# Weighted values of an attention kernel in 24 closed runs, and its output projection in three groups of rows

## The chip, the cores and the metric

The kernel runs on one core of a Trainium2 chip. Its engines are TensorE (PE for matrix products, PEld for the loads of their stationary operand), VectorE (DVE), ScalarE (ACT), GpSimd (POOL) and SyncE (SP, which issues most DMAs). Each executes its own queue in the order in which it was written, and engines wait for each other by semaphores. The metric is the device time of one execution in microseconds; smaller is better.

## The reference

Two layers of a decoder trunk over 512 tokens and 1024 features in float32. A layer is a gated feed-forward block, a mixer, and a second feed-forward block. The mixer's input projection feeds three groups of heads, whose outputs are concatenated and projected:

```python
x = x + 0.5 * swiglu(rmsnorm(x, ffn1_norm[l]), ...)
z = rmsnorm(x, mix_norm[l]) @ w_in[l]
y_s5, y_hg = s5_mixer(...), hgrn2_mixer(...)        # 256 + 256 columns
y_nsa = nsa_mixer(q_nsa, kv_nsa, gate_nsa, ...)     # 512 columns, 8 heads of 64 in 2 groups
y = jnp.concatenate([y_s5, y_hg, y_nsa], axis=-1)
x = x + y @ w_out[l]
x = x + 0.5 * swiglu(rmsnorm(x, ffn2_norm[l]), ...)
```

In `nsa_mixer` each block of 128 queries has three attentions (compressed keys, selected keys, a window), each softmax(q k + bias) times v, added with gates. With 512 tokens selection and window cover every earlier token, so both are causal attentions over blocks of 128 keys.

## The kernel before

Dense products keep precision by splitting: `mm3` (L222 to L226) makes a product of 128 by 512 from three matmuls, high weights times high input (L224), high weights times low input (L225), low weights times high input (L226). `wload` fetches a weight piece by an SP DMA into one of four `wraw` buffers; `wsplit` casts its high part on ACT (L218) and subtracts for the low part on DVE (L219), three buffers each. Products collect in PSUM tiles with the tag `pd`, of which there are two.

The program is written by Python generators which a small `Weave` interleaves; the framework's scheduler then orders the instructions of each engine. In `mixer`, `dense()` makes the input projection and starts the three head groups as their inputs come up; `outs()` works as filler beside them.

The attention is `nsa`. It has 16 units: group g (2), head pair hp (2) and query block i (4, of i+1 key blocks). I call the four units of one (g, hp) a half of a group. Each unit has three steps, and step `turn` comes two units behind `scores`, step `mix` three units behind (`LAG`):

- `scores`: four pairs of score matmuls into PSUM tiles with the tag `pS`, two buffers (L1154, L1155); on DVE bias plus minimum, L1158; on ACT exp, L1162; on DVE four small operations and the scaling by gate over sum, L1169.
- `turn`: i+1 transposes `ppt` for each of four probability tiles (L1178), and an ACT copy of each tile to `PT` (L1180).
- `mix`: 4(i+1) matmuls `pno` of values by transposed probabilities (L1194). Each uses 128 by 64 of the array and gives 64 rows; head e = 0 and e = 1 go to the two halves of the columns. After i = 3 one full matmul adds the compressed attention (L1197, called `pno.c` below), and `split` casts the half's output to its high part on ACT (L969) and takes the low part on DVE (L970). They are entries 4 to 7 of `self.y`; 0 and 1 come from the S5 heads, 2 and 3 from HGRN2.

The output projection `wout` goes over groups of entries of `self.y`, `WP = ((0, 1, 2, 3), (4, 5, 6, 7))`. For each of eight output tiles m it loads the piece of W for the group, makes three matmuls for each entry and adds PSUM to `x` on DVE (L1359). `outs` runs all groups but the last beside the head groups, each once its entries exist. The last runs when all generators are done, and also makes the next norm's sums and inputs (`norm_x`).

Of the kernel before, what the change touches and what calls it, by code (L numbers as in the profile page):

```python
# [19 lines left out]
L, DM, FF, DEPTH = 512, 1024, 2816, 2  # L20
# [37 lines left out]


GAP = 99.0  # L60


class Trunk:
# [13 lines left out]
    SB = (1.0, 1.5)  # L77
    S0 = 1
    ORD = ('h0', 'i', 's', 'h1', 'k0', 'v', 'c', 'k1')
    WP = ((0, 1, 2, 3), (4, 5, 6, 7))  # L80
    WW = 0.333
    CMPU = 2
    NW, HW, SW = 1.176, 0.84, 1.2
# [1038 lines left out]
    def nsa(self, st):  # L1122

        nc = self.nc
        v = nc.vector
        V, gates = st["v"], st["g"]
        T, pcT, po = {}, {}, {}
        units = [(g, hp, i) for g in range(2) for hp in range(2) for i in range(4)]

        def start(g):  # L1130
            while "k%d" % g not in st:
                yield 1.0
            T[g] = [self.bias_tile(4 * g + r) for r in range(4)]

        def cmp(g):
            while "vc" not in st:
                yield 1.0
            pcT[g] = yield from self.nsa_cmp(g, T[g], st["k%d" % g][1], st["kc"], gates)

        def scores(g, hp, i):  # L1140

            h = 4 * g + 2 * hp
            KS, Q = st["k%d" % g]
            n = 128 * (i + 1)
            nm = max(n, 256)
            qs = slice(i * 128, (i + 1) * 128)
            mx, sm_ = self.s([128, 4], "mx"), self.s([128, 4], "smx")
            P = [None] * 4
            for b in range(2):
                kh, kl = KS[b]  # L1150
                ps = [self.pmt(name="psS", tag="pS") for _ in range(2)]
                for e in range(2):

                    nc.tensor.matmul(ps[e][:, :nm], Q[2 * hp + e][:, qs], kh[:, :nm], start=True, stop=False)  # L1154
                    nc.tensor.matmul(ps[e][:, :nm], Q[2 * hp + e][:, qs], kl[:, :nm], start=False, stop=True)  # L1155
                for e in range(2):
                    p = P[2 * e + b] = self.t2(name="P")
                    v.tensor_tensor_reduce(p[:, :n], T[g][2 * hp + e][:, L - n:], ps[e][:, :n], 1.0, 1e29, OP.add,  # L1158
                                           OP.min, mx[:, 2 * e + b:2 * e + b + 1])
                yield 0.25 + 0.15 * i  # L1160
            for j in range(4):
                nc.scalar.activation(P[j][:, :n], P[j][:, :n], AF.Exp, bias=mx[:, j:j + 1], scale=-1.0,  # L1162
                                     accum_out=sm_[:, j:j + 1])
            v.tensor_scalar(sm_[:], sm_[:], TINY, None, op0=OP.max)
            v.reciprocal(sm_[:], sm_[:])
            v.tensor_tensor(sm_[:].rearrange("p (e b) -> p e b", e=2), sm_[:].rearrange("p (e b) -> p e b", e=2),
                            gates[:, i, 3 * h:3 * h + 6].rearrange("p (e k) -> p e k", e=2)[:, :, 1:3], op=OP.mult)
            for j in range(4):
                v.tensor_scalar(P[j][:, :n], P[j][:, :n], sm_[:, j:j + 1], None, op0=OP.mult)  # L1169
            return P  # L1170

        def turn(i, P):
            R = []
            n = 128 * (i + 1)
            for k in range(4):
                pt = self.pmt(name="ppt", tag=("pS", "pv")[k % 2])
                for j in range(i + 1):
                    nc.tensor.transpose(pt[:, j * 128:(j + 1) * 128], P[k][:, j * 128:(j + 1) * 128], self.idn[:])  # L1178
                PT = self.t2(name="PT")
                nc.scalar.copy(PT[:, :n], pt[:, :n])  # L1180
                R.append(PT)
                if k % 2:
                    yield 0.2 * (i + 1)
            return R

        def mix(g, hp, i, R):
            if i == 0:
                po[0] = self.pmt(name="pno", tag="po")
            qs = slice(i * 128, (i + 1) * 128)
            for b in range(2):  # L1190
                for j in range(i + 1):
                    c = slice(g * 128 + 64 * b, g * 128 + 64 * b + 64)
                    for e in range(2):
                        nc.tensor.matmul(po[0][64 * e:64 * e + 64, qs], V[:, j, c], R[2 * e + b][:, j * 128:(j + 1) * 128],  # L1194
                                         start=i == 0 and b == 0, stop=False, skip_group_check=True)
            if i == 3:
                nc.tensor.matmul(po[0][:], st["vc"][g][:, hp], pcT[g][:], start=False, stop=True, skip_group_check=True)  # L1197
                self.y[4 + 2 * g + hp] = self.split(po[0][:])
        P, R = {}, {}
        n = len(units)  # L1200
        lt, lm = self.LAG
        yield from start(0)
        nxt = {}
        for g in range(2):
            nxt[8 * g + self.CMPU] = cmp(g)
        nxt[self.K1] = start(1)
        run = []
        for k in range(n + lm):
            if k in nxt:
                run.append((k, nxt[k]))  # L1210
            for j, q in list(run):
                for _ in range(1 if k < j + 2 else 10 ** 6):
                    try:
                        yield next(q)
                    except StopIteration:
                        run.remove((j, q))
                        break
            if k < n:
                P[k] = yield from scores(*units[k])
            if 0 <= k - lt < n:  # L1220
                R[k - lt] = yield from turn(units[k - lt][2], P.pop(k - lt))
            if 0 <= k - lm < n:
                mix(*units[k - lm], R.pop(k - lm))
                yield 0.44 * (units[k - lm][2] + 1)


    def dense_tok(self, W, n, name, gates=None):
# [43 lines left out]
    def mixer(self, l, gi_next):  # L1271
        nc, A = self.nc, self.A
        with self.tc.tile_pool(name="mp%d" % l, bufs=self.NB) as mp:
# [29 lines left out]
                yield from self.s5_glu(l, y2)  # L1303

            def outs(n):
                for cs in self.WP[:n]:
                    while any(self.y[c] is None for c in cs):
                        yield 1.0
                    yield from self.wout(l, cs)

            def dense():
                for it in self.ORD:
# [30 lines left out]
            W.add(outs(len(self.WP) - 1), self.WW)  # L1343
            W.run()
            self.norm_start()
            drain(self.wout(l, self.WP[-1], True, gi_next))
        self.norm_end()

    def wout(self, l, cs, last=False, gi_next=None):
        nc = self.nc  # L1350
        n = len(cs)
        assert cs == tuple(range(cs[0], cs[0] + n))
        for m in range(KT):
            h, lo = self.wload(self.A["wo"][l, m][:, cs[0] * 128:(cs[0] + n) * 128], n * 128)
            ps = self.pmt(name="pd", tag="pd")
            for j, c in enumerate(cs):
                sl = slice(j * 128, (j + 1) * 128)
# [32 lines left out]
def _layout(inp):  # L1390
    a = {k: np.asarray(v) for k, v in inp.items()}
    r = {}
# [36 lines left out]
        return c(w.reshape(DEPTH, 128, KT * len(cols_)))  # L1429
    r["wvi"] = tok(HI + ar(256))  # L1430
    r["wvn"] = tok(np.concatenate([kvc(j, g) for g in range(2) for j in (3, 5)] + [GT + ar(24)]))
    r["wo"] = c(np.stack([tiles(a["w_out"][l], 128) for l in range(DEPTH)]).reshape(DEPTH, KT, 128, 1024))

    def cat(u, w):
        return np.concatenate([u, w], 0)
# [58 lines left out]
```

## Time and profile before

| | |
|---|---|
| median of 3 runs (range) | 2086.31 us (2082.22 to 2089.9) |
| profiled execution, its own time | 2082.53 us |
| its span | 2080.8 us |
| PE busy | 2051.0 us, 99% of the span |
| DVE, ACT busy | 57%, 38% |
| granted TensorE clock | 0.996 of full speed |

The span is the time from the first to the last instruction of the profiled execution; 1.7 us of its own time lie outside. Busy time is the union of an engine's instructions. PE matmuls are pipelined and their ends are modelled, so starts are more reliable than durations: what a matmul costs is read from its start to the start of the next one. A matmul of float32 operands with a 64-column array tile shows as two records; an average line can hide a stretch with other limits, so the stretches are read one by one.

### The profile page before, as it was taken

The page shows a single profiled execution, that of the slowest core. Times are in us where ns is not written, and L with a number is a line of the kernel's source. Part 1 is how long each engine was busy: PE and PEld are TensorE (multiplying, and loading weights), DVE is VectorE, ACT ScalarE, POOL GpSimd, SP SyncE. Part 2 cuts the span into 40 slices and gives each one's busy share as a digit, 9 for nine tenths or more (in the row PEclk, how much of TensorE's full clock was granted, in tenths as well). Part 3 has the DMA queues.
Part 4 walks back from the last instruction along what each step waited for, and adds up shares of the span by engine and source line. Part 5 has one row for each costly group of instructions (what it writes and reads, how often), then busy time and mean ns, then how long its engine had stood idle before and what let it go on. Part 6 is the DMA issues. An engine that isn't in the chain of part 4 may idle for free.

```text
span 2080.8 us, 28931 instructions
## 1 busy us (share of the span) xinstructions
PE 2051.0 (99%) x11192; PEld 1686.2 (81%) x11192; DVE 1188.5 (57%) x2653; ACT 782.2 (38%) x1455; POOL 83.4 (4%) x153
## 2 busy tenths in 40 slices
PE   8999999999999999999999999999999999999997
PEld 6888888877877888888888888888787778888886
DVE  7865545677776864543544344356777764344445
ACT  5322323445666332222332223234456663222221
POOL 1000000111000100000000000001110000000000
PEclk9999999999999999999999999999999999999999
DMA  5334433432102433432333233234221023233322
GB/s 194 110 103 138 133 130 94 151 126 97 52 26 63 142 114 94 151 95 80 110 101 89 84 114 99 80 105 151 99 97 52 32 87 91 86 97 112 97 78 69
DMA packets 69753, 209.11 MB, mean 100 GB/s; under 512 B 9272, under 2 KB 11912, under 8 KB 69616
## 3 DMA queue, kind: packets, MB, share of 16 engines
q1 hardware_dynamic: 58192, 172.19, 26.9%
q0 software_dynamic: 11280, 35.05, 4.9%
q8 instruction: 88, 1.44, 0.3%
q14 instruction: 49, 0.40, 0.1%
q10 hardware_dynamic: 144, 0.03, 0.0%
HBM read 194.63 MB, written 15.22 MB: 101 GB/s over the span
## 4 chain that ended last, share of the span: by engine, by line
PE 96%; DVE 2%; issue 0%; DMA 0%; ACT 0%; POOL 0%; SPq 0%; DVEq 0%; ACTq 0%
PE pd L224 27%; PE pd L226 27%; PE pd L225 27%; PE pno L1194 2%; PE ppt L1178 2%; PE psS L1154 1%; PE psS L1155 1%; PE pd L1246 1%; PE pd L1247 1%; PE pd L1248 1%; PE psc L1092 1%; PE plv L876 1%; PE pno L1197 0%; PE pho L942 0%; PE pY L784 0%
## 5 line engine op out<-in xcount | busy, mean ns | idle before, releaser
L218 ACT CAST whi<-wraw 128x1024 fp32r<-128x1024 f32 (+5 forms) x377 | 345.3, 918 | 1020.5 <-PE pd L225 713.8
L224 PE MATMUL pd<-xs,whi 128*128 128x512 f32 x1664 | 655.9, 394 | 9.6 <-ACT whi L218 6.1
L226 PE MATMUL pd<-xs,wlo 128*128 128x512 f32 x1664 | 652.0, 392 | 0.0
L225 PE MATMUL pd<-xs,whi 128*128 128x512 f32 x1664 | 650.4, 391 | 0.0
L219 DVE TENSOR_TENSOR wlo<-wraw,whi 128x1024 fp32r<-128x1024 f32 (+5 forms) x377 | 396.8, 1054 | 144.2 <-ACT whi L218 135.3
L224 PEld LDWEIGHTS pd<-xs,whi 128*128 128x128 f32 x1664 | 313.6, 188 | 77.2 <-ACT whi L218 6.1
L226 PEld LDWEIGHTS pd<-xs,wlo 128*128 128x128 f32 x1664 | 313.4, 188 | 65.4
L225 PEld LDWEIGHTS pd<-xs,whi 128*128 128x128 f32 x1664 | 313.5, 188 | 63.8 <-DVE xs L164 0.7
L224 PE MATMUL pd<-hb,whi 128*128 128x512 f32 x682 | 265.8, 390 | 0.0
L226 PE MATMUL pd<-hb,wlo 128*128 128x512 f32 x682 | 265.4, 389 | 0.0
L225 PE MATMUL pd<-hb,whi 128*128 128x512 f32 x682 | 265.4, 389 | 0.0
L293 DVE TENSOR_TENSOR ft<-ft,pd 128x512 f32<-128x512 f32 x88 | 60.5, 687 | 247.3 <-PE pd L226 247.0
L287 DVE TENSOR_TENSOR ft<-pd,rbc 128x512 f32<-128x512 f32 x88 | 60.7, 690 | 188.8 <-PE pd L226 188.8
L226 PEld LDWEIGHTS pd<-hb,wlo 128*128 128x128 f32 x682 | 128.0, 188 | 26.6
L225 PEld LDWEIGHTS pd<-hb,whi 128*128 128x128 f32 x682 | 128.1, 188 | 26.4
L224 PEld LDWEIGHTS pd<-hb,whi 128*128 128x128 f32 x682 | 128.1, 188 | 26.3
L312 DVE TENSOR_TENSOR ft<-pd,r 128x512 f32<-128x512 f32 x62 | 42.9, 692 | 109.7 <-PE pd L226 109.4
L1162 ACT ACTIVATE P<-P,mx 128x128 f32<-128x128 f32 (+3 forms) x128 | 71.4, 559 | 36.2 <-DVE mx L1158 35.0
L1158 DVE CUSTOM_DVE_ANT_0 P<-Tb,psS 128x128 f32<-128x128 f32 (+3 forms) x128 | 60.3, 483 | 21.0 <-PE psS L1155 20.1
L295 DVE TENSOR_TENSOR hb<-ft,hb 128x512 fp32r<-128x512 f32 x88 | 60.3, 685 | 0.0
L288 ACT ACTIVATE ft<-ft 128x512 f32<-128x512 f32 x88 | 55.1, 628 | 12.8 <-DVE ft L287 12.5
L294 ACT CAST hb<-ft 128x512 fp32r<-128x512 f32 x88 | 54.7, 622 | 13.0 <-DVE ft L293 11.1
(388 smaller groups left out, 2138.6 us busy)
## 6 DMA issues: line engine op xcount, KB each, us to landing
wraw<-in_gu SPq DMA_DIRECT2D x175, 512.0 KB, 3.5
wraw<-in_dn SPq DMA_DIRECT2D x64, 384.0 KB, 3.0
wraw<-in_dn SPq DMA_DIRECT2D x64, 320.0 KB, 2.8
wraw<-in_win SPq DMA_DIRECT2D x32, 512.0 KB, 3.6
w<-sp POOLq DMA_DIRECT2D x32, 256.0 KB, 5.7
wraw<-in_wo SPq DMA_DIRECT2D x32, 256.0 KB, 2.6
Tb<-tbl POOLq DMA_DIRECT2D x16, 256.0 KB, 4.2
tbl<-ext POOLq DMA_DIRECT2D x1, 2560.0 KB, 20.5
```

Of the source, the lines that this page charges most:

```text
L218: nc.scalar.copy(h[:, sl], w[:, sl])
L219: self.mark = nc.vector.tensor_tensor(lo[:, sl], w[:, sl], h[:, sl].bitcast(F32), op=OP.subtract)
L224: nc.tensor.matmul(ps, wh, xh, start=first, stop=False)
L225: nc.tensor.matmul(ps, wh, xl, start=False, stop=False)
L226: nc.tensor.matmul(ps, wl, xh, start=False, stop=last)
L287: nc.vector.tensor_tensor(t[:], pg[:], rbc[:], op=OP.mult)
L288: nc.scalar.activation(t[:], t[:], AF.Silu)
L293: nc.vector.tensor_tensor(t2[:], t[:], pu[:], op=OP.mult)
L294: nc.scalar.copy(hb[:, 0, f], t2[:])
L295: nc.vector.tensor_tensor(hb[:, 1, f], t2[:], hb[:, 0, f].bitcast(F32), op=OP.subtract)
L1158: v.tensor_tensor_reduce(p[:, :n], T[g][2 * hp + e][:, L - n:], ps[e][:, :n], 1.0, 1e29, OP.add, OP.min, mx[:, 2 * e + b:2 * e + b + 1])
L1162: nc.scalar.activation(P[j][:, :n], P[j][:, :n], AF.Exp, bias=mx[:, j:j + 1], scale=-1.0, accum_out=sm_[:, j:j + 1])
```

## The change

It has two parts.

1. `mix` now takes its `pno` matmuls in one closed run. Blocks i = 0 and 1 of a half go together (12 matmuls), i = 2 (12) and i = 3 (16) alone, so there are three runs in each of four halves of two layers. The matmuls have high priority in the scheduler, and a dependency without a semaphore orders the first behind all ACT copies of the run. Blocks 0 and 1 share their four `PT` tiles.
2. The output projection has three groups, `((0, 1), (4, 5), (2, 3, 6, 7))`, and the rows of its weights are stored in that order. The first needs the S5 heads alone, the second the attention's group 0; the last group keeps four entries.

```diff
-    WP = ((0, 1, 2, 3), (4, 5, 6, 7))
+    WP = ((0, 1), (4, 5), (2, 3, 6, 7))
...
         def turn(i, P):
...
+            o = 128 if i == 1 else 0
+            if i != 1:
+                PT[:] = [self.t2(name="PT") for _ in range(4)]
...
-                PT = self.t2(name="PT")
-                nc.scalar.copy(PT[:, :n], pt[:, :n])
-                R.append(PT)
+                c = nc.scalar.copy(PT[k][:, o:o + n], pt[:, :n])
+                R.append((PT[k], o, c.ins.name))
...
-        def mix(g, hp, i, R):
+        def mix(g, hp, blocks):
...
+            with self.tc.high_priority():
+                for i, R in blocks.items():
...
+                                mm.append(nc.tensor.matmul(po[0][64 * e:64 * e + 64, qs], V[:, j, c],
...
+                for R in blocks.values():
+                    for _, _, c in R:
+                        self.tc.add_manual_dep(mm[0].ins, c, NOSYNC, reason="one run")
...
-            if 0 <= k - lm < n:
-                mix(*units[k - lm], R.pop(k - lm))
-                yield 0.44 * (units[k - lm][2] + 1)
+            if 0 <= k - lm < n and units[k - lm][2]:
+                g, hp, i = units[k - lm]
+                bl = (0, 1) if i == 1 else (i,)
+                mix(g, hp, {j: R.pop(k - lm + j - i) for j in bl})
+                yield 0.44 * sum(j + 1 for j in bl)
...
-    def wout(self, l, cs, last=False, gi_next=None):
+    def wout(self, l, q, last=False, gi_next=None):
...
+        cs = self.WP[q]
+        n, o = len(cs), sum(len(g) for g in self.WP[:q])
         for m in range(KT):
-            h, lo = self.wload(self.A["wo"][l, m][:, cs[0] * 128:(cs[0] + n) * 128], n * 128)
+            h, lo = self.wload(self.A["wo"][l, m][:, o * 128:(o + n) * 128], n * 128)
```

The diff does not show where the scheduler puts the instructions. In the rows below `psS` are score matmuls (`kh` the first of a pair, `kl` the second), `ppt` transposes, `pno` matmuls of values, `pd<-y` the output projection, `psc` scores of the compressed attention; `x4` is the number of equal instructions in a row. The changed kernel's lines are some 1 to 20 further down: L1154 and L1155 become L1155 and L1156, L1178 becomes L1183, L1194 becomes L1203, L1197 becomes L1211.

The first place is PE in the second half of group 0, layer 0. Before:

```order
L1194 MATMUL pno<-PT,vn 64x128
L1178 MATMUL ppt<-idn,P 128x128 x8
L1194 MATMUL pno<-PT,vn 64x128 x11
L1092 MATMUL psc<-kc,q 128x7 x4
L1178 MATMUL ppt<-idn,P 128x128
L1194 MATMUL pno<-PT,vn 64x128
L226 MATMUL pd<-y,wlo 128x512
L1154 MATMUL psS<-kh,q 128x384
L1155 MATMUL psS<-kl,q 128x384
L1178 MATMUL ppt<-idn,P 128x128
L1194 MATMUL pno<-PT,vn 64x128 x2
```

The same half now, at its first run (the fourth of the layer's twelve):

```order
L1156 MATMUL psS<-kl,q 128x512
L1183 MATMUL ppt<-idn,P 128x128 x4
L225 MATMUL pd<-y,whi 128x512
L226 MATMUL pd<-y,whi 128x512
L227 MATMUL pd<-y,wlo 128x512
L1203 MATMUL pno<-PT,vn 64x128 x12
L1155 MATMUL psS<-kh,q 128x256
L1156 MATMUL psS<-kl,q 128x256
```

Pieces of one to eleven `pno` between other matmuls became one run of twelve, five rows behind the last score matmul of block 3.

The second place is ACT in the same half, whose copies the run needs. Before:

```order
L1162 ACTIVATE P,smx<-P,mx 128x512 x4
L1180 COPY PT<-ppt 128x256 x4
L218 CAST whi<-wraw 128x512
L1162 ACTIVATE P,smx<-P,mx 128x128 x4
L1180 COPY PT<-ppt 128x384 x4
```

Now:

```order
L219 CAST whi<-wraw 128x256
L1163 ACTIVATE P,smx<-P,mx 128x512 x4
L1184 COPY PT<-ppt 128x256 x2
L1163 ACTIVATE P,smx<-P,mx 128x128 x4
L1184 COPY PT<-ppt 128x384 x4
L1163 ACTIVATE P,smx<-P,mx 128x256 x4
L1184 COPY PT<-ppt 128x512 x4
```

The order of exps and copies on ACT hardly moved: two of the four copies of 256 columns, all four of 384 and all four of 512 still stand behind four exps of a later block.

The third place is PE at the end of the attention, layer 0. Before:

```order
L224 MATMUL pd<-y,whi 128x512
L225 MATMUL pd<-y,whi 128x512
L1178 MATMUL ppt<-idn,P 128x128 x12
L1194 MATMUL pno<-PT,vn 64x128 x8
L1178 MATMUL ppt<-idn,P 128x128 x16
L1194 MATMUL pno<-PT,vn 64x128 x28
L1197 MATMUL pno<-pcT,vc 128x512
L226 MATMUL pd<-y,wlo 128x512
```

Now:

```order
L1155 MATMUL psS<-kh,q 128x512
L1156 MATMUL psS<-kl,q 128x512
L1183 MATMUL ppt<-idn,P 128x128 x4
L1203 MATMUL pno<-PT,vn 64x128 x12
L1183 MATMUL ppt<-idn,P 128x128 x12
L1203 MATMUL pno<-PT,vn 64x128 x12
L1183 MATMUL ppt<-idn,P 128x128 x10
L1203 MATMUL pno<-PT,vn 64x128 x16
L1211 MATMUL pno<-pcT,vc 128x512
L225 MATMUL pd<-y,whi 128x512 x2
```

The 28 `pno` behind 16 transposes became runs of 12 and 16, each right behind transposes, and the first run stands four transposes behind the last score matmul.

## Rows read from the trace of the kernel before

**Rows 1.** The page's head and part 1: busy time, share of span, instructions.

```profile
span 2080.8 us, 28931 instructions
...
PE 2051.0 (99%) x11192; PEld 1686.2 (81%) x11192; DVE 1188.5 (57%) x2653; ACT 782.2 (38%) x1455; POOL 83.4 (4%) x153
```

**Rows 2.** Windows: stretch, length, busy us of PE, PEld, DVE, ACT, POOL, clock, DMA.

```profile
540.00:660.00 120.00, 120.00 (x852) 93.44 (x850) 82.79 (x355) 77.53 (x258) 2.14 (x4) 1.00 0.11 35
...
584.05:606.24 22.19, 22.19 (x175) 17.18 (x174) 16.65 (x69) 14.98 (x50) 0.00 (x0) 1.00 0.06 22
```

**Rows 3.** Waits of PE, longest in total first: us, times, longest.

```profile
PE pd L224 <- ACT whi L218: 6.1, 1, 6.1
```

**Rows 4.** Timeline of PE around two runs of values: start us, us, instruction.

```profile
561.91 0.28 PE L1154 MATMUL psS<-kh,q 128*128 128x256 f32 x1
562.03 0.28 PE L1155 MATMUL psS<-kl,q 128*128 128x256 f32 x1
562.24 1.09 PE L1194 MATMUL pno<-PT,vn 128*64 128x128 f32 x14
563.26 0.50 PE L224 MATMUL pd<-y,whi 128*128 128x512 f32 x1
563.60 0.40 PE L225 MATMUL pd<-y,whi 128*128 128x512 f32 x1
563.84 0.40 PE L226 MATMUL pd<-y,wlo 128*128 128x512 f32 x1
...
566.69 0.43 PE L1194 MATMUL pno<-PT,vn 128*64 128x128 f32 x2
567.05 0.50 PE L224 MATMUL pd<-y,whi 128*128 128x512 f32 x1
```

**Rows 5.** Timeline, the last block of the attention: last score, fourth exp, first copy.

```profile
646.45 0.39 PE L1155 MATMUL psS<-kl,q 128*128 128x512 f32 x1
...
647.64 0.71 ACT L1162 ACTIVATE P<-P,mx 128x512 f32<-128x512 f32 x1
...
648.35 0.35 ACT L1180 COPY PT<-ppt 128x256 f32<-128x256 f32 x1
```

**Rows 6.** Groups by line and shape: count | busy us, mean ns | idle before.

```profile
L1180 ACT COPY PT<-ppt 128x512 f32<-128x512 f32 x32 | 16.4, 597 | 1.8 <-PE ppt L1178 1.8
...
L1180 ACT COPY PT<-ppt 128x384 f32<-128x384 f32 x32 | 13.0, 493 | 0.1
...
L1180 ACT COPY PT<-ppt 128x256 f32<-128x256 f32 x32 | 10.0, 371 | 3.8 <-PE ppt L1178 3.8
```

**Rows 7.** Timeline, a block of 256 keys: last score, fourth exp, copies behind it.

```profile
575.22 0.28 PE L1155 MATMUL psS<-kl,q 128*128 128x256 f32 x1
...
576.05 0.49 ACT L1162 ACTIVATE P<-P,mx 128x256 f32<-128x256 f32 x1
...
576.54 2.03 ACT L1180 COPY PT<-ppt 128x512 f32<-128x512 f32 x4
```

**Rows 8.** Timeline, a block of 128 keys: last score and fourth exp.

```profile
571.07 0.28 PE L1155 MATMUL psS<-kl,q 128*128 128x256 f32 x1
...
571.94 0.39 ACT L1162 ACTIVATE P<-P,mx 128x128 f32<-128x128 f32 x1
```

**Rows 9.** Timeline of PE, the last 16 transposes and the 28 `pno` behind.

```profile
651.26 1.97 PE L1178 MATMUL ppt<-idn,P 128*128 128x128 f32 x16
653.16 3.28 PE L1194 MATMUL pno<-PT,vn 128*64 128x128 f32 x56
```

**Rows 10.** Timeline, from the attention's last matmul to the output projection of entry 7.

```profile
656.37 1.12 PE L1197 MATMUL pno<-pcT,vc 128*128 128x512 f32 x2
...
657.58 0.59 ACT L969 CAST y<-pno 128x512 fp32r<-128x512 f32 x1 [3.57 <-PE pno L1197]
...
658.25 0.70 PE L224 MATMUL pd<-y,whi 128*128 128x512 f32 x2
```

**Rows 11.** Groups by line and shape: the addition of the output projection to x.

```profile
L1359 DVE TENSOR_TENSOR x<-x,pd 128x512 f32<-128x512 f32 x32 | 21.7, 684 | 9.4 <-PE pd L226 9.1
```

More of the change, by code (lines that the diff above doesn't have):

```diff
@@ L60 @@
 GAP = 99.0
+NOSYNC = mybir.DependencyInfo(mybir.DependencyClass.NoSync, mybir.DependencyReason.DATA)
 class Trunk:
@@ L1184, in turn @@
             return R
-        def mix(g, hp, i, R):
-            if i == 0:
+        def mix(g, hp, blocks):
+            if 0 in blocks:
                 po[0] = self.pmt(name="pno", tag="po")
[L1189 to L1197, printed above, removed]
+            mm = []
+            with self.tc.high_priority():
+                for i, R in blocks.items():
+                    qs = slice(i * 128, (i + 1) * 128)
+                    for b in range(2):
+                        for j in range(i + 1):
+                            c = slice(g * 128 + 64 * b, g * 128 + 64 * b + 64)
+                            for e in range(2):
+                                t, o, _ = R[2 * e + b]
+                                mm.append(nc.tensor.matmul(po[0][64 * e:64 * e + 64, qs], V[:, j, c],
+                                                           t[:, o + j * 128:o + (j + 1) * 128],
+                                                           start=i == 0 and b == 0, stop=False, skip_group_check=True))
+                for R in blocks.values():
+                    for _, _, c in R:
+                        self.tc.add_manual_dep(mm[0].ins, c, NOSYNC, reason="one run")
+                if 3 in blocks:
+                    nc.tensor.matmul(po[0][:], st["vc"][g][:, hp], pcT[g][:], start=False, stop=True,
+                                     skip_group_check=True)
+            if 3 in blocks:
                 self.y[4 + 2 * g + hp] = self.split(po[0][:])
+        PT = []
         P, R = {}, {}
@@ L1305, in outs @@
             def outs(n):
-                for cs in self.WP[:n]:
+                for q, cs in enumerate(self.WP[:n]):
                     while any(self.y[c] is None for c in cs):
                         yield 1.0
-                    yield from self.wout(l, cs)
+                    yield from self.wout(l, q)
             def dense():
@@ L1345, in mixer @@
             self.norm_start()
-            drain(self.wout(l, self.WP[-1], True, gi_next))
+            drain(self.wout(l, len(self.WP) - 1, True, gi_next))
         self.norm_end()
-    def wout(self, l, cs, last=False, gi_next=None):
+    def wout(self, l, q, last=False, gi_next=None):
         nc = self.nc
-        n = len(cs)
-        assert cs == tuple(range(cs[0], cs[0] + n))
+        cs = self.WP[q]
+        n, o = len(cs), sum(len(g) for g in self.WP[:q])
         for m in range(KT):
-            h, lo = self.wload(self.A["wo"][l, m][:, cs[0] * 128:(cs[0] + n) * 128], n * 128)
+            h, lo = self.wload(self.A["wo"][l, m][:, o * 128:(o + n) * 128], n * 128)
             ps = self.pmt(name="pd", tag="pd")
@@ L1431, in _layout @@
     r["wvn"] = tok(np.concatenate([kvc(j, g) for g in range(2) for j in (3, 5)] + [GT + ar(24)]))
-    r["wo"] = c(np.stack([tiles(a["w_out"][l], 128) for l in range(DEPTH)]).reshape(DEPTH, KT, 128, 1024))
+    wo = np.stack([tiles(a["w_out"][l], 128) for l in range(DEPTH)])
+    r["wo"] = c(wo[:, :, :, [q for g in Trunk.WP for q in g]].reshape(DEPTH, KT, 128, 1024))
     def cat(u, w):
```

2 lines of the change are left out of this document (1 added, 1 removed).

## The prediction

> **What bounds the kernel now.** I read the page first. PE is busy for 2051.0 of 2080.8 us [rows 1], so a term counts only if it shortens PE's own work or makes PE wait. Then the windows: the attention of layer 0 lies at 540 to 660 us, layer 1 repeats it some 1027 us later, and PE is busy there for 120.00 of 120.00 us while DVE is busy for 82.79 and ACT for 77.53 [rows 2]. Then PE's waits: the longest is 6.1 us at the program's start, and no entry of that list names a copy `PT` [rows 3]. So in the attention PE never waits visibly; what it can save is inside its own stream, and the timeline shows what that is.
>
> **What a run of values costs.** Seven `pno` matmuls show as 14 records and take from 562.24 to 563.26 us, 1.02 us; one matmul, two records, takes from 566.69 to 567.05, 0.36 us [rows 4]. Heads e = 0 and 1 overlap, so I count slots of two matmuls: the first run has four, the second one. A slot is then (1.02 - 0.36) / 3 = 0.22 us, and 0.14 us of a run depends on nothing. Beside this, the score matmul ahead takes 0.21 us to the run's start where its like takes 0.12 (561.91 to 562.03), 0.09 more; the dense matmul behind takes 0.34 us (563.26 to 563.60) where the next takes 0.24, 0.10 more [rows 4]. A run costs 0.33 us apart from its slots. These lie in full on PE, which sets the end.
>
> The rows also show what changes there: matmuls on 128 by 128 of the array, then on 128 by 64, then back [rows 4]. The Trainium skill, "TensorEngine Tiling (Array Packing)", Key Properties, says that changing the tiling mode drains the engine, and "TensorE: Matmul & The Clock Gate", Part 2, gives a drain as some 128 cycles, which is 0.05 us at 2.4 GHz. By that figure, an estimate, a run would cost 0.11 us for its two changes, and the change would save 5 instead of 15 us on them. The sum goes by the rows.
>
> **What is saved.** In the order of PE I count 35 runs in each layer before, of 1 to 28 matmuls; 90 slots, since a lone or odd matmul fills a slot as a pair does. Now there are 12 runs and 80 slots. A layer saves 23 x 0.33 = 7.6 us and 10 x 0.22 = 2.2 us; both layers 19.6 us. Bounds: if the runs' price were only 0.14 + 0.09 us (the exit hidden under the next matmul) it would be 15; a gain above 20 has no row for it.
>
> **What is new: the run waits for its last copy.** Before, `pno` came in pieces once copies were long made, and filled the time of scores, exps and copies. Now a run stands as early as its copies allow, and a single late copy holds up PE with everything queued behind it: scores, transposes and filler alike. Most late copies stand on ACT behind four exps of a later block. I take the time from the start of that block's last score matmul on PE to the end of the last copy, and compare it with the PE work that the new order puts between that matmul and the run.
>
> - Behind exps of 512 columns: 1.19 us to the fourth exp, 0.71 for it [rows 5], two copies of 256 at 10.0 / 32 = 0.31 [rows 6]: 2.5 us. PE's work between, at 0.23 for a dense or 512-column matmul [rows 4], 0.11 for a transpose (16 in 1.90 us less the 0.09 [rows 9]) and 0.09 to enter: for run 4 of the layer 0.23 + 0.44 + 0.69 + 0.09 = 1.4 us; run 7 has 1.9, run 10 only 0.75. Waits: 1.1, 0.6 and 1.75 us.
> - Behind exps of 128 columns: 0.87 + 0.39 us [rows 8] and four copies of 384 at 0.41 [rows 6], 2.9 us; the exp seen there may have queued behind others, so I take 2.75. Work between for runs 2, 5 and 8: 2.35, 1.45 and 2.55. Waits: 0.4, 1.3, 0.2.
> - Behind exps of 256 columns: 0.83 + 0.49 + 2.03 us [rows 7], 3.35. Work between for runs 3, 6 and 9: 2.9, 2.3 and 2.9. Waits: 0.45, 1.05, 0.45.
> - Run 1 has its copies just behind its last transposes and much dense work, 0.2. Run 11 starts late enough after run 10's wait, none. Run 12 stands right behind ten transposes whose tiles take 0.51 us each to copy [rows 6] and 0.44 to transpose: 0.8.
>
> A layer waits 8.3 us, both 16.6. Bounds: if the copies were always ready, nothing; but each sum is of strict dependencies in queue order, so I see no row for less than half of it. Above, each can grow by queueing.
>
> **What moves: the output projection.** The 192 matmuls of a layer stay the same. Entry 7 now finds all 18 dense matmuls that need not wait for it used up as filler; 14 were before. After the attention's last matmul the ACT cast starts 1.21 us later and the first product of entry 7 at 1.88 us [rows 10]; the matmul itself takes 1.07, so PE waits 0.8 us per layer. The second group needs entry 5, whose cast stands on ACT behind four exps of 384 and four copies of 128 of the next block. Scores, minimum, exps, copies and cast add up to some 4.8 us where PE has 4.0 us of work, and the low part comes 0.7 us after: I take 1.4 us per layer. Both items, both layers: 4.4 us; nothing if the filler falls better, 8 if the next matmuls stall as well.
>
> Eight more pieces per layer mean eight more SP DMAs, casts, subtractions, and additions to x of 0.68 us [rows 11]. That is 5.5 us more on DVE, which has 37 idle us in the attention's 120, while the DMA engines are used to 11% [rows 2]; I cost them at nothing. If that cover were gone, each layer would lose up to those 5.5 us. `PT` tiles are fewer by 16 per layer, while entries 2 and 3 live longer: nothing.
>
> **Sum.** 2082.5 (the profiled execution's own time) - 19.6 + 16.6 + 4.4 = 2083.9 us, 1.4 us more. That execution stands 3.8 us below the median of the runs; against the median 2086.3 this is 2087.7, and I forecast **2087.5 us**, no change that can be told. A measurement of this kernel can tell about 0.5%, or 10.4 us, from no change.
>
> **The rivals.**
>
> *The waits are hidden, and the kernel is faster.* For it: DVE and ACT have slack in the stretch [rows 2], and before not one wait for a copy is seen. If only the runs with little dense filler ahead (4, 5, 6, 10, 12) wait, 6.0 us per layer, and entries 5 and 7 are covered, the time is 2086.3 - 19.6 + 12.0 = 2078.7; if nothing waits, 2066.7. It is faster by over 0.5% once a layer loses less than 4.6 us in all. Against it: the queue order of exps and copies is fixed and every price is from a row. Chance 0.18 for passing that point.
>
> *The score matmuls wait for PSUM, and it is slower.* The pieces of `pno` also kept score matmuls apart. There are two `pS` buffers, and a third pair in a row must wait until DVE has read the first. In the second half of group 0 four pairs of 256 and later four of 384 columns follow nearly without anything between; A buffer is free about when its exp can start, 1.19 us after the pair's second matmul starts [rows 5]; with 0.23 for the first, two buffers let a pair pass every 0.71 us, where it takes 0.46 itself: 0.25 us of wait. If 24 of a layer's 64 pairs wait, this is 6 us per layer, 2087.5 + 12.0 = 2099.5. It decides from 4.5 us per layer, 18 pairs; in the order I count about 12 that follow so closely. The Trainium skill, "TensorEngine Tiling (Array Packing)", PSUM Bottleneck, warns that tiling speeds up TensorE but not the reading of PSUM, which would then bound. Against it: DVE was busy for 16.65 and ACT for 14.98 of 22.19 us in that half [rows 2], so neither is full on average. Chance 0.18.
>
> *The change doesn't close the runs* is excluded: the order shows 24 runs of 12 and 16.
>
> **How the numbers follow.** Forecast 0.64, the two rivals 0.18 each: faster 0.18, same 0.64, slower 0.18. The forecast's own spread is the waits' half (-8) to a few more us of queueing (+8). The range reaches some way into both rivals: 2076 to 2099.
>
> **What would show it.** In the profile after, `pno` should stand in 24 runs, with idle time of PE ahead of runs 4, 5, 6 and 10, 1 to 2 us each, released by `PT` copies; the attention's stretch should keep its length within 3 us, while PE does its work in some 10 us less. The forecast is wrong if these gaps are absent (then near 2070), or if gaps ahead of `psS`, released by DVE's minimum, add up to more than those ahead of `pno`.

## The result, and the profile after

The changed kernel takes **2097.62 us** (median of 4 runs, 2096.73 to 2102.47), the kernel before on the same chip 2085.18 us (4 runs, 2082.22 to 2089.9). The ratio is estimated at 1.0065 with an interval of 1.0046 to 1.0083 (the two medians divide to 1.0060): it is slower by some 0.65%, a little more than the 0.5% that can be told from no change. The range held; the likeliest case, no change, did not come.

The page's first lines, of the profiled execution after:

```profile
span 2100.7 us, 29050 instructions
...
PE 2061.1 (98%) x11192; PEld 1693.4 (81%) x11192; DVE 1197.9 (57%) x2685; ACT 782.8 (37%) x1471; POOL 83.0 (4%) x153
```

Against [rows 1] PE is busy 10 us longer, though its work was to shrink, and it is idle in another 10. Both lie in one place. I cut each profile at the norm sums `pss`, between which the head groups and most of the output projection of a layer lie. First the windows of that stretch before, layer 0 and layer 1. Columns: window, its length, busy us (and instructions) of PE, PEld, DVE, ACT, POOL, granted clock, DMA share, GB/s.

```profile
384.10:680.80 296.70, 291.85 (x2291) 235.09 (x2290) 217.65 (x651) 166.85 (x430) 25.26 (x45) 0.99 0.26 85
1411.10:1707.80 296.70, 291.83 (x2291) 235.10 (x2290) 217.56 (x651) 166.81 (x430) 22.84 (x40) 0.99 0.26 84
```

The same two stretches after, and then, in order of time, every stretch within them in which the granted clock stood at half:

```profile
384.50:690.50 306.00, 295.77 (x2291) 238.47 (x2290) 222.40 (x667) 167.32 (x438) 25.13 (x44) 0.97 0.26 82
1420.20:1727.80 307.60, 296.58 (x2289) 238.48 (x2289) 222.42 (x667) 167.12 (x438) 22.71 (x40) 0.97 0.26 81
462.40:465.80 3.40, 3.36 (x60) 3.24 (x62) 3.40 (x7) 1.91 (x4) 0.00 (x0) 0.50 0.02 5
472.60:476.00 3.40, 3.40 (x14) 2.98 (x12) 3.06 (x7) 2.88 (x6) 0.00 (x0) 0.50 0.02 5
612.60:619.40 6.80, 6.80 (x23) 5.52 (x23) 3.85 (x18) 3.25 (x13) 0.00 (x0) 0.50 0.00 0
650.10:653.50 3.40, 3.40 (x13) 2.70 (x12) 3.26 (x10) 1.99 (x6) 0.00 (x0) 0.50 0.00 0
1500.00:1503.40 3.40, 3.40 (x53) 2.96 (x48) 3.40 (x9) 1.86 (x5) 0.00 (x0) 0.50 0.02 5
1510.30:1520.50 10.20, 10.20 (x40) 9.36 (x39) 3.74 (x10) 3.35 (x8) 0.91 (x1) 0.50 0.07 27
1653.60:1657.00 3.40, 3.40 (x11) 2.52 (x11) 2.54 (x15) 2.31 (x11) 0.00 (x0) 0.50 0.00 0
```

The two stretches are 9.3 and 10.9 us longer; the rest of the program keeps its length (1487.4 us before, 1487.1 after). The 20.2 us fall into three parts, and this division carries everything below:

- **Idle time of PE** (length less busy): 4.85 and 4.87 us before, 10.23 and 11.02 after: +11.5 us.
- **The clock.** Half clock stood for 17.0 us in each layer after, for 3.4 in each before (471.0 to 474.4 and 1498.4 to 1501.9). Half of such time is lost, so 8.5 and 1.7 us a layer: +13.6 us.
- **PE's busy time at full clock** (busy less what the clock took): 290.1 us a layer before, 287.3 and 288.1 after: -4.9 us.

So the waits and PE's work together cost 6.6 us, and the clock in this execution 13.6. The profiled execution is the slowest of the four, at a mean clock of 0.989. The other three have 0.993, so by (1 - clock) times span they lose 14.7 us to it where the profiled one loses 23.1 and the one before 8.3 (0.996). Against the profiled execution before, they lose 6.4 us more. The clock of the four runs of before isn't known, but their median stands 2.7 us above that execution, and of the 23 runs of before beside e1 (below) the seven above 2086 us have clocks of 0.991 to 0.994. So of the 12.4 us between the medians some 4 to 6 are clock, and the rest is idle time net of the work saved; the clock has three digits, so this is good to a microsecond or two.

PE's waits after, longest in total first: us, times, longest.

```profile
PE ppt L1183 <- DVE mx L1159: 3.0, 13, 0.5
...
PE psc L1093 <- ACT PT L1184: 2.3, 4, 0.7
...
PE psS L1155 <- ACT PT L1184: 1.9, 4, 0.6
PE pd L225 <- ACT y L970: 1.4, 2, 0.7
PE psS L1155 <- DVE mx L1159: 1.1, 6, 0.2
PE pd L225 <- DVE x L1379: 1.0, 4, 0.3
...
PE ppt L1183 <- ACT PT L1184: 0.6, 2, 0.3
...
PE pno L1203 <- ACT PT L1184: 0.2, 1, 0.2
```

In the list before, which [rows 3] begin, only the one of `pd` for x stands, with 0.6. Ahead of the runs, where I looked for 1 to 2 us each, PE waits 0.2 us in total. It waits ahead of transposes (`ppt`), scores (`psS`) and compressed scores (`psc`): 3.0 + 2.3 + 1.9 + 1.1 + 0.6 = 8.9 us, 4.5 per layer. These three share the PSUM buffers with the tag `pS`: a unit's scores ask for them in twos, every second transposed tile (L1181) and the compressed scores for one each, and there are two. A score matmul that is released by a copy `PT` waits for the buffer of the transposes that this copy empties; a transpose that is released by DVE's minimum waits for the buffer of the scores that it reads.

The timeline of PE after shows the places: start us, us, instruction, in brackets the idle time ahead of it and what ended it.

```profile
599.55 1.53 PE L1203 MATMUL pno<-PT,vn 128*64 128x128 f32 x24
601.01 0.39 PE L1155 MATMUL psS<-kh,q 128*128 128x256 f32 x1
601.24 0.28 PE L1156 MATMUL psS<-kl,q 128*128 128x256 f32 x1
601.36 0.28 PE L1155 MATMUL psS<-kh,q 128*128 128x256 f32 x1
...
609.35 0.45 PE L1155 MATMUL psS<-kh,q 128*128 128x384 f32 x1 [0.19 <-DVE mx L1159]
...
610.62 0.80 PE L1183 MATMUL ppt<-idn,P 128*128 128x128 f32 x2 [0.18 <-DVE mx L1159]
612.11 1.50 PE L1093 MATMUL psc<-kc,q 128*128 128x15 f32 x8 [0.68 <-ACT PT L1184]
...
617.11 0.63 PE L1155 MATMUL psS<-kh,q 128*128 128x512 f32 x1
617.54 0.63 PE L1156 MATMUL psS<-kl,q 128*128 128x512 f32 x1
...
620.01 0.40 PE L226 MATMUL pd<-y,whi 128*128 128x512 f32 x1
620.24 0.39 PE L227 MATMUL pd<-y,wlo 128*128 128x512 f32 x1
...
647.57 0.44 PE L1155 MATMUL psS<-kh,q 128*128 128x384 f32 x1 [0.20 <-DVE mx L1159]
...
648.85 0.33 PE L1183 MATMUL ppt<-idn,P 128*128 128x128 f32 x1 [0.47 <-DVE mx L1159]
649.74 0.50 PE L1155 MATMUL psS<-kh,q 128*128 128x512 f32 x1 [0.56 <-ACT PT L1184]
...
657.08 0.66 PE L1203 MATMUL pno<-PT,vn 128*64 128x128 f32 x8
657.90 1.36 PE L1203 MATMUL pno<-PT,vn 128*64 128x128 f32 x16 [0.16 <-ACT PT L1184]
...
667.92 0.73 PE L225 MATMUL pd<-y,whi 128*128 128x512 f32 x2 [0.68 <-ACT y L970]
```

The run at 599.55 is clean: 1.46 us to the next start, and six slots at 0.22 plus 0.14 are 1.46, as in [rows 4]. Of the 24 runs after, 20 take just this price, to 0.01 us; only runs 10 and 12 of each layer are longer, by 0.65 and 0.35 us. So for copies at or in the runs PE waits 2.0 us in all. At 617 the clock is at half and a step takes 0.43 us, at 620 it takes 0.23. From 647.57 to 649.74 PE waits three times within 2.2 us, with no dense matmul between; 0.4 us later the clock falls. Run 10 (657.08) does wait for its copies, but inside: the dependency orders only the run's first matmul and has no semaphore.

### The profile page after: what moved, and what is told of

Read it like the earlier page. It is cut to its first block, busy times and chain, and to the rows that moved or that the text cites. A ratio compares the mean times of both kernels' runs of the same rounds, so it can differ in the third digit from the quotient of the medians.

```text
span 2100.7 us, 29050 instructions
## 1 busy us (share of the span) xinstructions
PE 2061.1 (98%) x11192; PEld 1693.4 (81%) x11192; DVE 1197.9 (57%) x2685; ACT 782.8 (37%) x1471; POOL 83.0 (4%) x153
## 4 chain that ended last, share of the span: by engine, by line
PE 93%; DVE 2%; issue 2%; ACT 2%; DMA 0%; POOL 0%; SPq 0%; DVEq 0%; ACTq 0%; POOLq 0%
PE pd L225 27%; PE pd L227 26%; PE pd L226 26%; PE pno L1203 2%; PE ppt L1183 2%; PE psS L1155 1%; ACT P L1163 1%; PE psS L1156 1%; PE psc L1093 1%; PE pho L943 1%; PE pd L1265 1%; PE plv L877 1%; PE pd L1266 1%; PE pd L1267 1%; DVE P L1159 0%
## 5 line engine op out<-in xcount | busy, mean ns | idle before, releaser
L219 ACT CAST whi<-wraw 128x1024 fp32r<-128x1024 f32 (+4 forms) x393 | 348.3, 888 | 1017.2 <-PE pd L226 697.6
L220 DVE TENSOR_TENSOR wlo<-wraw,whi 128x1024 fp32r<-128x1024 f32 (+4 forms) x393 | 398.4, 1017 | 144.4 <-ACT whi L219 135.2
L1183 PE MATMUL ppt<-idn,P 128*128 128x128 f32 x320 | 55.6, 286 | 4.3 <-DVE mx L1159 3.0
```

Source lines behind the costliest of these rows:

```text
L219: nc.scalar.copy(h[:, sl], w[:, sl])
L220: self.mark = nc.vector.tensor_tensor(lo[:, sl], w[:, sl], h[:, sl].bitcast(F32), op=OP.subtract)
```

## The experiments

Two questions: which part of the change costs the time, the runs or the groups, and what PE waits for, the copies (my forecast) or the `pS` buffers (the second rival). A PSUM bank that another tag (`pT`) holds could be moved without changing the sum of banks, which gave a direct trial. "Of after" and "of before" say which kernel an edit starts from. The results of all are in one table; idle, busy at full clock and half clock are us of the stretch between the norm sums in the profiled execution, layer 0 / layer 1. The ratios are estimated against runs of before beside each series (medians 2082.42 to 2085.18 us), and aren't quotients of the table's medians.

| kernel | median us (range, runs) | ratio to before (interval) | idle | busy at full clock | at half clock |
|---|---|---|---|---|---|
| before | 2085.18 (2082.22 to 2089.9, 4) | | 4.9 / 4.9 | 290.1 / 290.1 | 3.4 / 3.4 |
| after | 2097.62 (2096.73 to 2102.47, 4) | 1.0065 (1.0046 to 1.0083) | 10.2 / 11.0 | 287.3 / 288.1 | 17.0 / 17.0 |
| e1 runs only | 2085.14 (2083.31 to 2089.66, 10) | 1.0 (0.9987 to 1.0013) | 9.3 / 9.8 | 286.2 / 286.1 | 3.4 / 17.0 |
| e2 groups only | 2094.93 (2092.11 to 2099.09, 7) | 1.0042 (1.0025 to 1.006) | 6.5 / 7.4 | 291.4 / 292.1 | 10.2 / 3.4 |
| e3 after, third `pS` | 2072.81 (2072.46 to 2076.61, 5) | 0.9942 (0.9923 to 0.9961) | 6.6 / 6.1 | 282.1 / 282.1 | 6.8 / 13.7 |
| e4 before, third `pS` | 2077.67 (2075.57 to 2084.77, 10) | 0.9982 (0.9972 to 0.9992) | 4.4 / 4.5 | 287.5 / 287.4 | 3.4 / 3.4 |
| e5 runs later | 2089.54 (2088.34 to 2097.06, 10) | 1.0026 (1.0014 to 1.0039) | 11.0 / 11.5 | 286.6 / 286.9 | 17.0 / 6.8 |
| e6 runs only, third `pS` | 2071.82 (2071.15 to 2072.65, 4) | 0.9949 (0.9934 to 0.9963) | 5.9 / 6.2 | 283.6 / 283.4 | 3.4 / 3.4 |
| e7 as e6, last half in pieces | 2071.2 (2068.89 to 2075.11, 4) | 0.9947 (0.9933 to 0.9962) | 6.8 / 7.0 | 282.4 / 282.4 | 3.4 / 3.4 |
| e8 other groups | 2096.85 (2093.36 to 2098.94, 4) | 1.0072 (1.0055 to 1.0089) | 10.9 / 10.7 | 286.7 / 287.1 | 10.2 / 6.8 |
| e9 other groups, later | 2090.14 (2089.61 to 2095.61, 4) | 1.0039 (1.0024 to 1.0054) | 10.7 / 11.3 | 287.8 / 288.1 | 3.4 / 3.4 |
| e10 after, third `pd` | 2101.05 (2100.56 to 2101.37, 4) | 1.0085 (1.007 to 1.0101) | 11.0 / 11.0 | 290.1 / 290.1 | 6.8 / 6.8 |
| e11 as e7, runs later | 2069.81 (2069.26 to 2072.18, 4) | 0.9939 (0.9923 to 0.9956) | 6.1 / 6.1 | 280.0 / 279.5 | 6.8 / 10.2 |
| e12 after, third `pv` | 2097.9 (2094.13 to 2101.45, 6) | 1.0057 (1.0038 to 1.0077) | 10.9 / 10.3 | 287.7 / 287.0 | 10.2 / 17.0 |

**e1, the closed runs alone** (of after):

```diff
-    WP = ((0, 1), (4, 5), (2, 3, 6, 7))
+    WP = ((0, 1, 2, 3), (4, 5, 6, 7))
```

> The change's closed runs with the two groups of the output projection as they were. Theory A (the closed runs take away the small pieces of PE work that stood between scores, transposes and copies, and PE then waits for PSUM buffers and copies): about as slow as the full change, 2093 to 2100 us, with the last half of group 1 at 17 to 20 us between its two pno.c where before had 14.4. Theory B (the second half of group 0 lost its filler because the first group of the projection has only two entries): most of the loss is gone, 2070 to 2082 us.

Measured 2085.14 us, ratio 1.0: no change, between the two numbers I had set, so neither theory holds as it stands. The sign named for theory A did come: the last half of group 1 takes 19.1 and 20.7 us between its two `pno.c` (the second with 3.4 us at half clock). The stretches of e1:

```profile
383.70:680.90 297.20, 287.92 (x2291) 233.30 (x2290) 217.39 (x651) 166.10 (x430) 25.09 (x44) 0.99 0.27 84
1410.60:1715.00 304.40, 294.56 (x2289) 238.96 (x2289) 217.30 (x651) 166.13 (x430) 22.79 (x40) 0.97 0.26 82
```

In layer 0, at the same clock as before, PE is busy 3.9 us less and idle 4.4 us more. The runs give back as waits what they save. This profiled execution was the slowest of the ten, at a clock of 0.993 where most had 0.995 or 0.996, and its layer 1 shows why: the same work there takes 7.2 us longer, of which 6.8 are half clock.

**e2, the three groups alone** (of before): the second part of the change's diff and nothing of the first.

```diff
-    WP = ((0, 1, 2, 3), (4, 5, 6, 7))
+    WP = ((0, 1), (4, 5), (2, 3, 6, 7))
```

> The three groups of the output projection alone, values in pieces as before. Theory A: within 4 us of the kernel before, 2081 to 2089 us. Theory B: slower by 8 us or more, 2093 or above, with waits in the second half of group 0.

Measured 2094.93 us, ratio 1.0042: the groups by themselves are slower, though most of the work that they move was not to touch the path. Without the clock the table gives 1.6 + 2.5 us more idle and 1.3 + 2.0 us more busy than before, 7.4 in all; the rest of the 11 us that separate it from the runs of before beside it (2083.55, 2082.03 to 2090.92, 23 runs) is mostly half clock, 10.2 us of it in layer 0. Part of the busy time is again the values: among the moved filler they fall into 41 runs a layer (88 slots), where before has 35 (90), which at 0.33 and 0.22 us is 1.5 us more a layer. The second group also waits for entry 5 here, 0.47 and 0.78 us for its low part, and the compressed scores wait 0.7 us a layer for the copies that free their buffer.

**e3 and e4, a third `pS` buffer** (of after, and of before):

```diff
-    PB = {"pd": 2, "pS": 2, "pT": 1, "po": 1, "pv": 2}
+    PB = {"pd": 2, "pS": 3, "po": 1, "pv": 2}
...
-        pre.append(drain(self.dense_x(self.A["gu"][fi, 2, 0], tag="pT")))
+        pre.append(drain(self.dense_x(self.A["gu"][fi, 2, 0], tag="pv")))
```

> The full change with three pS buffers of PSUM instead of two (the bank of a tile that only the start used). Theory A1 (the waits are for PSUM buffers that score tiles and transposes share): the waits of ppt, psS and psc fall by more than half and the time comes to 2080 to 2089 us. Theory A2 (the waits are for exps and copies in ACT's order, whatever the buffers): they move to ahead of the runs, and the time stays within 3 us of the change, 2094 to 2100 us.

> The kernel before with three pS buffers and nothing else. If PSUM buffers only matter once the values are in closed runs: within 3 us of before, 2081 to 2087 us, since before shows no wait for them in the attention. If a third buffer helps any order: about 10 us faster, near 2073.

The changed kernel falls to 2072.81 us, by 25, below the 2080 to 2089 that theory A1 had set, and is now faster than before (0.9942). The kernel before gains only some 4 to 6 us from the same bank (0.9982), between the two cases set for it. The stretches of e3, and then those of e4:

```profile
384.60:676.70 292.10, 285.53 (x2289) 234.96 (x2288) 219.99 (x667) 166.62 (x438) 25.09 (x45) 0.99 0.28 86
1406.60:1701.60 295.00, 288.93 (x2288) 238.14 (x2288) 219.99 (x667) 166.47 (x438) 22.84 (x40) 0.98 0.26 84
```

```profile
384.60:678.20 293.60, 289.16 (x2289) 235.31 (x2288) 216.00 (x651) 165.36 (x430) 25.15 (x45) 0.99 0.27 86
1408.40:1702.00 293.60, 289.14 (x2289) 235.22 (x2288) 215.80 (x651) 165.36 (x430) 22.83 (x40) 0.99 0.27 85
```

Leaving the clock out, the third buffer takes 8.8 and 10.9 us from the layers of after, and 3.1 from each of before. So two buffers cost the changed kernel 19.7 - 6.2 = 13.5 us more than they cost the old one. Of what the buffer takes from after, 5.2 and 6.0 us a layer are time in which PE counted as busy, with the same work in the same 12 runs; so part of the waiting seems to lie inside PE's records, where the list of waits doesn't show it. (Of before's 6.2 us two runs a layer fewer, 33 for 35, explain 1.3.) In the source nothing but the number of buffers (and the place of one product at the start of a feed-forward block) differs; the scheduler's order of PE differs with it, as it does in e10, which gains nothing. So the wait for `pS` buffers, the second rival's mechanism, is shown for the whole change; how much of it the runs alone bring is worked out below. What is left of the waits in e3:

```profile
PE psS L1155 <- DVE cmx L1097: 1.1, 2, 0.6
PE psS L1155 <- ACT PT L1184: 1.1, 2, 0.6
...
PE pct L1111 <- DVE pc L1106: 0.4, 2, 0.2
PE ppt L1183 <- DVE mx L1159: 0.3, 2, 0.2
PE psc L1093 <- DVE mx L1159: 0.3, 2, 0.2
```

Of the 8.9 us ahead of transposes and scores 2.8 stay; the wait of scores for `cmx` is for a buffer of the compressed scores, the same tag.

**e5, each run later** (of after): every run also stands behind the last transpose of the next unit, by a dependency without a semaphore; the last two runs of the layer's last half fall together (11 runs a layer).

```diff
-                    nc.tensor.transpose(pt[:, j * 128:(j + 1) * 128], P[k][:, j * 128:(j + 1) * 128], self.idn[:])
+                    last_t[0] = nc.tensor.transpose(pt[:, j * 128:(j + 1) * 128], P[k][:, j * 128:(j + 1) * 128], self.idn[:]).ins.name
...
+                self.tc.add_manual_dep(mm[0].ins, last_t[0], NOSYNC, reason="behind the next unit's transposes")
```

> The full change, with each run also ordered behind the transposes of the next unit, so that PE has 8 to 16 transposes more between a unit's copies and its run. Theory A2: the waits shrink, 2083 to 2091 us. Theory A1: transposes need PSUM tiles earlier, so that it is no better, 2095 to 2105 us.

Measured 2089.54 us, 1.0026, a time in the range of theory A2. The profile doesn't bear that theory out. Against after idle time does not fall (11.0 and 11.5 us) and busy time falls by about 1: to let copies finish earlier relative to their run does not remove the waits in this execution, with two `pS` buffers. Of the 8 us that it is faster than after, some 4 are clock (eight of its ten runs have 0.995, after 0.993); for the rest its profiled execution, with 2097.06 us the slowest of the ten, gives no reason, and this stays open.

**e6, the runs alone with a third `pS`** (both edits above).

> Closed runs and three pS buffers, with the two groups of the output projection as before. If the three groups cost about 10 us also with three buffers: 2060 to 2065 us. If the third buffer took away what the groups cost too: 2070 to 2075 us, like the change with three buffers.

Measured 2071.82 us, 0.9949, beside e3's 2072.81. With a third buffer the groups cost nothing that can be told. Its stretches:

```profile
384.10:675.30 291.20, 285.29 (x2291) 233.56 (x2290) 215.16 (x651) 165.19 (x430) 25.14 (x45) 0.99 0.27 86
1405.10:1696.40 291.30, 285.14 (x2289) 233.56 (x2289) 215.01 (x651) 165.32 (x430) 22.86 (x40) 0.99 0.27 85
```

Against e4, at the same clock and with the same buffers, closing the runs is worth 2.4 and 2.3 us a layer: 3.9 us less of busy time, 1.5 to 1.7 more idle (e4 has 33 runs a layer, this one 12).

**e7, the last half of the layer in pieces** (of e6): in the half g = 1, hp = 1 no priority and no dependency on all copies. Its values then stand in runs of 4, 8 and 28 matmuls, as at the end of before, so the number of runs stays 12.

```diff
-            with self.tc.high_priority():
+            last = g == 1 and hp == 1
+            with (ExitStack() if last else self.tc.high_priority()):
...
-                for R in blocks.values():
+                for R in ([] if last else blocks.values()):
```

> The same, with the last half of group 1 in pieces again, where no filler is left. If the last runs of a layer wait for their copies at a loss (the stretch before had 14.4 us, with runs 17.9 to 19.1): 5 to 8 us faster than the kernel with all runs closed. If the stretch is long for another cause: the same.

Measured 2071.2 us, 0.9947: the same as e6, where one theory had asked for 5 to 8 us. The last half does get shorter, from 17.5 to 16.6 us between its two `pno.c` (14.4 before), but 0.9 us a layer is below what the runs can tell.

**e8 and e9, other groups** (of after): the second group takes entries 2 and 3 instead of the attention's 4 and 5, so no group but the last waits for the attention; in e9 both groups also start only once entries 0 to 3 exist.

```diff
-    WP = ((0, 1), (4, 5), (2, 3, 6, 7))
+    WP = ((0, 1), (2, 3), (4, 5, 6, 7))
...
-                    while any(self.y[c] is None for c in cs):
+                    while any(self.y[c] is None for c in (0, 1, 2, 3) + cs):
```

> The full change with two pS buffers, its three groups being entries 0 and 1, 2 and 3, 4 to 7, so that none but the last waits for the attention. If the groups cost time because filler is held back until entry 5 exists: near the runs alone, 2083 to 2088 us. If they cost it because eight more pieces a layer are loaded, split and added: as slow as the change, 2094 to 2100 us.

> Two pS buffers, groups of entries 0 and 1, 2 and 3, 4 to 7, but the first group waits until entries 2 and 3 exist too, as it did before the change. If the groups cost time because the first one starts early and its filler is gone when it is wanted: 2083 to 2088 us, like the runs alone. If it is the eight more pieces a layer, each with an addition on DVE: still 2092 to 2099 us.

e8 is as slow as after (2096.85), so the wait for entry 5 is not what the groups cost. e9 takes 2090.14, between its two ranges, which reads like a half of their cost returned by a later start. Its stretches say otherwise:

```profile
384.10:684.30 300.20, 289.54 (x2289) 233.46 (x2289) 221.81 (x667) 167.08 (x438) 25.19 (x45) 0.99 0.26 84
1414.00:1715.10 301.10, 289.84 (x2291) 233.55 (x2290) 221.71 (x667) 167.09 (x438) 22.74 (x40) 0.99 0.26 83
```

Idle and busy time at full clock are no smaller than in e8 (298.5 and 299.4 us together against 297.6 and 297.8). What differs is the clock: three of e9's four runs have 0.996, e8's have 0.990 to 0.993. The one run of e9 at 0.993 took 2095.61 us, the one of e8 at 0.993 2093.36. At the same clock there is no gain.

**e10 and e12, the bank elsewhere** (of after): a third buffer for the products `pd`, or for `pv`, which the other half of the transposes use.

```diff
-    PB = {"pd": 2, "pS": 2, "pT": 1, "po": 1, "pv": 2}
+    PB = {"pd": 3, "pS": 2, "po": 1, "pv": 2}
...
-    PB = {"pd": 2, "pS": 2, "pT": 1, "po": 1, "pv": 2}
+    PB = {"pd": 2, "pS": 2, "po": 1, "pv": 3}
```

> The full change, the spare PSUM bank given to the pd tiles (three) and not to pS (two). If pieces wait for their pd tile until DVE has added it to x: most of what a third pS buffer gave, 2075 to 2085 us. If only the buffers that scores and transposes share hold PE up: 2092 to 2098 us.

> The full change, the spare PSUM bank given to the pv tiles (three), which take every second transpose tile, and pS left at two. If transposes hold PE up for want of a tile of either kind: about half of what a third pS buffer gave, 2080 to 2090 us. If it is the score tiles' own two buffers: 2094 to 2101 us.

2101.05 us (above both ranges) and 2097.9: neither helps, and with `pd` PE's busy time grows by 2 to 3 us a layer. The product at the start of a feed-forward block is moved in both as in e3, so that isn't the gain either. So e3's gain is not that of any further bank; it is that of `pS`.

**e11, the best version**: e7 with the later runs of e5.

> Three pS buffers, two groups, runs behind the next unit's transposes, the last half of group 1 in pieces. If the runs still wait for copies with three buffers: 3 to 6 us faster than without the later place, 2065 to 2069 us. If the buffers were all: the same, 2070 to 2073 us.

Measured 2069.81 us, 0.9939 (0.9923 to 0.9956), between the two ranges. It is the fastest median of the series and beats both kernels, but its interval overlaps those of e3, e6 and e7. Its stretches:

```profile
384.10:673.60 289.50, 283.42 (x2288) 234.69 (x2288) 215.01 (x651) 165.04 (x430) 25.39 (x45) 0.99 0.27 87
1403.70:1694.40 290.70, 284.56 (x2288) 235.67 (x2288) 215.72 (x651) 165.05 (x430) 22.56 (x40) 0.98 0.27 86
```

Without the clock it takes 286.1 and 285.6 us a layer, 5.8 and 6.3 less than e4 and 3.1 to 3.8 less than e7. Half clock, 6.8 and 10.2 us of it, takes part of that back. That by the profiles a later run helps here and not in e5 points again to the buffers: the copies are waited for where nothing else is. As e5's medians leave some 4 us open, this isn't shown.

## Why the prediction was right or wrong

**What is saved (-19.6 us).** The price of a run held: all 35 runs of a layer before and 20 of the 24 after take 0.14 us beside their slots, to 0.01; into the run at 599.55 the last transpose takes 0.20 us, 0.09 more than its like, and the score matmul behind it 0.23 (601.01 to 601.24) where the next takes 0.12. The saving never showed whole. With three buffers and late runs, where least is waited for, e11 lies 12.1 us below e4, though its last halves aren't closed: it has 13 runs and 81 slots a layer where e4 has 33 and 90. The prediction weighed 0.33 us a run against 0.11, an estimate from the drain of some 128 cycles in the Trainium skill, "TensorE: Matmul & The Clock Gate", Part 2. By 0.11 at most 20 x 0.11 + 2.0 = 4.2 us a layer, 8.4 in all, could be saved. e11's 12.1, with waits still in it, speaks for the price of the rows.

**The runs' waits (+16.6 us): the step that failed.** I had PE wait for the last copy at the runs. The sign that I named, gaps of 1 to 2 us ahead of runs 4, 5, 6 and 10, is absent: 0.2 us in total ahead of `pno`, and with the time inside runs 10 and 12 it is 2.0 us after, 2.4 in e1 (runs 9, 10 and 12). The other sign that I named for being wrong is there: gaps ahead of `psS` exceed those ahead of `pno`, and with transposes and compressed scores they are 8.9 us. PE waits for a `pS` buffer, not at the runs. That the amount came near is luck. Runs alone (e1) come out at +0.5 and +0.9 us a layer without the clock, +1.4, where the terms gave 16.6 - 19.6 = -3.0; if the 19.6 was saved in full, 21.0 us are waited. Of these, 9.4 are seen as more idle time of PE and 2.4 inside runs; the rest would be inside other records, which isn't shown. With the third buffer (e6 against e4, whose runs and slots ask for a saving of 18.3) 18.3 - 4.7 = 13.6 us are left, of which 3.2 are seen as idle time and 3.2 inside runs 9 to 12; the others aren't placed. So copies are waited for as well, and how much each takes depends on the other.

**The output projection (+4.4 us).** Entry 7: 0.8 us forecast, 0.68 measured at 667.92; e1 has the same 0.68, so it comes with the runs, not the groups. Entry 5: 1.4 us per layer forecast, none seen after, 0.47 and 0.78 in e2. The eight pieces more, costed at nothing: PE waits for additions to x for 1.0 us after and 3.0 in e9, where before it was 0.6. Without the clock the groups add 2.0 and 3.2 us to e1, 5.2 in all: the size of the term, from other causes. With a third `pS` (e3 against e6) they are 0.8 and 1.4 us a layer better than none, so most of what they cost is again the two buffers. Which of the moved pieces uncovers which wait stays open; e8 and e9 exclude entry 5 and the early start.

**The second rival was put aside with 0.18.** "In the order I count about 12 that follow so closely" counted pairs of scores against pairs of scores. The transposes and the compressed scores use the same two buffers, and they follow scores more closely still. The argument "neither is full on average" was about the busy share of DVE and ACT, while the wait is one of latency: a buffer is held for scores, minimum or copy in turn, however idle these engines are otherwise. The price of 0.25 us took a buffer to be held until the fourth exp starts ([rows 5]); what releases PE after is DVE's minimum or a copy. I priced the rival at 12.0 us with 6 a layer, and two buffers cost 13.5 us more than before, 6.7 a layer, beyond its point of decision of 4.5. But that is the whole change. With the runs alone, of which the rival speaks, two buffers cost 12.3 us (e1 against e6), 6.1 more than before, 3.0 a layer: short of that point, and e1 is no slower than before. The other 7.4 come with the groups, which the rival doesn't name.

**What the sum lacked: the clock.** No term stood for it. It accounts for some 4 to 6 us of the 12.4 between the medians, and for 13.6 of 20.2 in the profiled execution. Without it the profiled kernel would stand 6.6 us above the one before, within what I had called no change. These 6.6 are 1.4 from the runs and 5.2 from the groups, where the sum had -3.0 and +4.4. That 2097.62 lies in the range is in part luck: its upper end was drawn to reach into the second rival, and the time came there by half of that rival's wait, by the groups and by the clock.

## What to carry to other kernels

Small pieces of work that look like overhead may be what keeps two users of one PSUM tag apart: before closing them into a run, list by tag, not by name, what will stand next to each other, and count buffers for that. If PE's waits after a change name releasers of several kinds (a copy, a minimum) ahead of instructions that share a tag, move one bank to that tag before touching the order; here that was worth 25 us, the change itself minus 12. And divide a difference into idle, busy and clock before explaining it: e9 would have passed for a gain of 7 us by a later start.

## What the hardware showed that was not expected

The granted clock fell to the lower of its two levels (0.50 of 2.4 GHz) in stretches in which PE was hardly idle: in layer 0 after, PE was busy for 78.00 of the 83.07 us between the first `pno.c` and the last (583.05 to 666.12), and the clock fell there at 612.6 and 650.1. Ahead of the fall at 650.1 PE waited 0.20, 0.47 and 0.56 us within 2.2 us; ahead of the one at 612.6 it waited 0.19, 0.18 and 0.68 us (609.35 to 612.11). Between the first `pno.c` of a layer and its last the profiles of before, e4, e6, e7, e9 and e11 show no such fall, those of after and the other seven do; e11 has two shortly ahead of the first, at 563.7 and 1584.3. The Trainium skill, "TensorE: Matmul & The Clock Gate", describes this under "A second HAM failure mode: psum-queue depth-cycling": cycling through PSUM banks makes PE idle briefly and often, and its clock goes back and forth between the two levels. The falls at 612.6 and 650.1 agree; e9, with 10.7 us of idle time against 10.2 in layer 0 of after and no fall between its first `pno.c` and its last, shows that the amount of idle time alone doesn't decide. Most of the rest, up to 10.2 us at half clock in one piece, lies ahead of the attention and changes from layer to layer of one execution (e1: 3.4 and 13.6 us). Executions of the kernel before differ as well: of 23 four had a clock of 0.991 and took up to 2090.92 us. What sets it is open; each kernel has one profile only.
